# A blocked fast-multiplication kernel: five more operand pairs split a second time, A read in longer runs, and its first block weighed while it is staged

## The chip, the cores and the metric

The kernel runs on one core of a Trainium2 chip. The metric is device time in microseconds of one execution. Before the change it is 1574.9 us, the median of three runs (1574.21 to 1575.22). The profile shown below is of one further execution; its span is 1572.0 us.

The engines are named as in the profile: PE is TensorE (PEld its weight loads), DVE is VectorE, ACT is ScalarE, POOL is GpSimd, SP is SyncE.

## The reference

```python
def setup_inputs():
    m, k, n = 4096, 4096, 4096
    return {"a": np.random.randn(m, k).astype(np.float32),
            "b": np.random.randn(k, n).astype(np.float32)}

def reference(a, b):
    x = np.matmul(a, b)
    return 0.5 * x * (1 + np.tanh(np.sqrt(2 / np.pi) * (x + 0.044715 * x**3)))
```

A product of two 4096 x 4096 matrices, followed by the tanh form of GELU. Input and output are float32.

## The kernel before

A and B are cut in half both ways, into quadrants 11, 12, 21 and 22. Seven products of sums of quadrants (a Strassen scheme) give the four quadrants of the result, in place of eight. Everything is cast to float16 by the DMA that loads it; sums are accumulated in float32 in PSUM. The output is made in 16 groups: four blocks of rows of A (`mb`), each with four blocks of columns of B (`nb`). One group needs the seven products M1 to M7, each of 512 x 512 outputs over a depth of 2048. A product is done in four steps `q`, a step being 16 matmuls of 128 x 512:

```python
PRODUCTS = [   # name, chain of PSUM banks, operand of A, operand of B
    ("M3", "Y", "11", ("12", "22", 1)),
    ("M5", "X", ("11", "12", -1), "22"),
    ("M7", "X", ("12", "22", -1), ("21", "22", 1)),
    ("M1", "X", ("11", "22", -1), ("11", "22", -1)),
    ("M4", "X", "22", ("21", "11", 1)),
    ("M2", "Y", ("22", "21", -1), "11"),
    ("M6", "Y", ("21", "11", -1), ("11", "12", 1)),
]
```

In some groups a pair of products (M3 with M5, or M2 with M1) is split once more: the product's two operand blocks are cut in quarters, and seven products of quarter sums take the place of eight. One such small product is one step of 16 matmuls of 128 x 256 (with two of 128 x 512 in one of the seven). `FRESH` is the order of the seven products in groups where M2 and M1 are split. `SPLITS` says which groups split which pair:

```python
SPLIT = {"1": ("11", ("11", "22", -1), ("11", "22", -1)), "3": ("12", "11", ("12", "22", 1)), ...}
PAIR = [(s, p) for ps in ("213", "45", "76") for s in (0, 1) for p in ps]   # 14 steps, two chains in turn
SPLITS = {M3_M5: (11, 13, 14, 15), M2_M1: (13, 14)}

def multiply_split(gi, s, p):
    ...
    for r in range(RT // 2):
        ...
        for j in range(NJ):                                   # 2 x 8 matmuls
            wide = p == "2" and j == 0
            nc.tensor.matmul(
                banks[chain, i][:, :] if wide else out,
                sa[:, j // 2, r * P : (r + 1) * P, j % 2],
                sb[:, : NC] if wide else sb[:, j * NC // 2 : (j + 1) * NC // 2], ...)
    ...
    # joins of the small products: DVE additions and ACT copies of 128 x 256 float32
```

The split needs operands of its own. Of B, the quarter sums are made once for each column block in the group `maker[nb]`, written to DRAM (`k_split`) and fetched back by POOL's DMA in later groups (tile `bK`, 1 MB each). Of A, first the block's sum (`aD`, four DVE additions of 128 x 2048), then the quarters' sums from it (`aS`, one addition each). The instructions of each engine stand in the order in which this code records them; a `step` is the unit of this schedule, and lists such as `before[n]` and `tasks[n]` say what is recorded just before step `n`.

```python
def block_sum(gi, s, o, q):        # aD <- aT, aT
def operand_a(gi, s, q, tag):      # aS <- aD, aD  or  aS <- aT, aT
def make_split(gi, name, p):       # bS <- bK, bK, then keep_operand -> k_split in DRAM
    ...
            if block and q == PAIR[0][1]:                     # the four sums of a block, all in one step
                e = max(ready, last_a, *(e for _, e in places[s]))
                for qq in range(QPH):
                    task(e, block_sum, gi, s, oa, qq)
```

A is loaded into one of two buffers `stage`, in runs of 256 elements of a row, and turned by DVE's 32 x 32 transpose into `aT`. It is also weighed: the kernel takes the sums of squares of the rows of A (and of columns of B) to find out at the end whether float16 was safe; a general path stands behind it if not. ACT does this, one row of a tile at a time, with the squares written to a scrap tile. A block for later groups is staged by `stage_block` within the last group that uses the block before it (groups 3, 7 and 11). The first block is not weighed when it is loaded; it is read a second time for that, from group 9 on:

```python
a_v = a.rearrange("(x mm) (c g r) -> c g mm x r", mm=Q, g=4, r=RUN)      # RUN = 256

def load_a(mb, quad, c, h=None):
    s = pool.tile([P, NX, RUN], F16, name="stage", tag="stage", bufs=2)
    return [(s[g * Q : (g + 1) * Q, x : x + n, :], a_v[kh * CH + c, g, :, x0 : x0 + n, :]) for g in range(4)]

def weigh_rows(mb, quad, c, xs):
    for x in xs:
        nc.scalar.activation(weighed[mb, quad, c][:, :RUN], s[:, x, :], ACT.Square,
                             accum_out=weighed[mb, ih][:, k, x : x + 1])

def stage_block(mb, turns, turned=True):
    for (quad, c), n in zip(chunks, turns):
        do(max(n - LOAD_AHEAD, free_at.pop(0)), load, (load_a, (mb, quad, c)))   # LOAD_AHEAD = 6 steps
        do(n, turn_a, mb, quad, c)
        for x in range(3):
            do(n + 1 + x, weigh_rows, mb, quad, c, ...)
stage_block(0, [first_step[CHECK_GROUP] + 8 + 6 * x ...], turned=False)           # CHECK_GROUP = 9
```

At the start, group 0 runs on whatever has been loaded: 16 steps of plain products of quadrants (`plain`), then the second halves of M3, M5, M7 and so on. 46 matmuls on zeros (`warm`) come ahead of it. ACT copies finished sums out of PSUM in between: `keep("x1", ...)`, the tile `c21`, and `keep("m5", ...)`. The order of the loads and turns of the first block is a table:

```python
for n, whats in (
    (0, "A11_0 B12_0 T11_0 B11_0 A21_0 A12_0 B22_0 B21_0"),    # A, B: load; T: turn
    (4, "T21_0 A22_0"), (6, "T12_0"), (8, "A11_1+B12_1+B22_1"), (9, "T22_0 A12_1+B21_1a B21_1b"),
    (14, "T11_1 A22_1 B11_1"), (16, "T12_1 A21_1"), (18, "S2 S3 T22_1"), (23, "T21_1"),
):
```

Of the kernel before, what the change touches and what calls it, by code (L numbers as in the profile page):

```python
# [16 lines left out]
P = 128  # L17
# [45 lines left out]

MAKES = (("M3", (1, 0)), ("M5", (2, 1)), ("M1", (4, 0)), ("M2", (5, 3)))
M3_M5, M2_M1 = 0, 3
PLACE = {"M3": (M3_M5, 0), "M5": (M3_M5, 1), "M2": (M2_M1, 0), "M1": (M2_M1, 1)}
SPLIT_AHEAD = 6
FETCH_AHEAD = 12
SPLITS = {M3_M5: (11, 13, 14, 15), M2_M1: (13, 14)}
LOAD_AHEAD = 6  # L70
CHECK_GROUP = 9

TURNS = ((2, 2), (3, 3), (5, 2), (6, 2), (8, 0), (9, 0), (10, 2), (11, 2))
# [58 lines left out]
def half_path(  # L132
# [26 lines left out]
    checks = {which: iter(range(stats[which].shape[1] // NX)) for which in stats}  # L159

    a_v = a.rearrange("(x mm) (c g r) -> c g mm x r", mm=Q, g=4, r=RUN)
    b_v = b.rearrange("(c g jj q e) n -> c g e q jj n", g=4, q=Q, e=2, jj=NJ // 2)
# [6 lines left out]
    def load_a(mb, quad, c, h=None):  # L169

        ih, kh = int(quad[0]) - 1, int(quad[1]) - 1
        n = NX if h is None else NX // 2
        x = 0 if h is None else h * n
        x0 = (ih * MH + mb * TM) // Q + x
        if not h:
            s = pool.tile([P, NX, RUN], F16, name="stage", tag="stage", bufs=2)
            staged[mb, quad, c] = s
        s = staged[mb, quad, c]
        return [
            (s[g * Q : (g + 1) * Q, x : x + n, :], a_v[kh * CH + c, g, :, x0 : x0 + n, :])  # L180
            for g in range(4)
        ]

    def turn_a(mb, quad, c, h=None):
        if not h:
            t = pool.tile([P, NJ // 2, TM * 2], F16, name="aT", tag=f"aT{a_slot[quad]}{c}")
            a_tiles[mb, quad, c] = t
        s, t = staged[mb, quad, c], a_tiles[mb, quad, c]
        x = slice(0, NX) if h is None else slice(h * NX // 2, (h + 1) * NX // 2)
        src = s.bitcast(U32).rearrange("p mb (jj q) -> p jj mb q", q=Q)  # L190
        dst = t.bitcast(U32).rearrange("p jj (mb q) -> p jj mb q", q=Q)
        nc.vector.transpose(dst[:, :, x, :], src[:, :, x, :])  # L192
        if h != 0 and mb == 0:
            del staged[mb, quad, c]

    def load_b(nb, quad, c, h=None):
        kh, jh = int(quad[0]) - 1, int(quad[1]) - 1
        n0 = jh * NH + nb * NC
        if not h:
# [5 lines left out]
            (t[g * Q : (g + 1) * Q, e::2, :], b_v[kh * CH + c, g, e, :, :, n0 : n0 + NC])  # L205
# [23 lines left out]
    def weigh_rows(mb, quad, c, xs):  # L229

        ih, kh = int(quad[0]) - 1, int(quad[1]) - 1
        s = staged[mb, quad, c]
        if (mb, ih) not in weighed:
            weighed[mb, ih] = pool.tile([P, 2 * CH, NX], F32, name="rows", tag="rows")
        if xs[0] == 0:
            weighed[mb, quad, c] = pool.tile([P, RUN], BF16, name="scrap", tag="scrap")
        for x in xs:
            k = kh * CH + c
            nc.scalar.activation(  # L239
                weighed[mb, quad, c][:, :RUN], s[:, x, :], ACT.Square, accum_out=weighed[mb, ih][:, k, x : x + 1]  # L240
            )
        if xs[-1] == NX - 1:
            del weighed[mb, quad, c], staged[mb, quad, c]

    def weigh_half(mb, ih):
        k, t = next(checks["a"]), weighed.pop((mb, ih))
        nc.vector.tensor_reduce(
            out=stats["a"][:, k * NX : (k + 1) * NX],
            in_=t.rearrange("p k x -> p x k"), axis=AX.X, op=ALU.add,
        )  # L250

# [16 lines left out]
    def weigh():  # L268

        for half in sorted(energy):  # L270
            k, t = next(checks["b"]), energy[half]
# [27 lines left out]
    def verdict(row):  # L299

        t = pool.tile([P, RUN], BF16, name="verdict", tag="scrap").bitcast(F32)[0:1, :]
# [30 lines left out]
    def product(gi, s):  # L332
        if gi == len(groups) - 1:
            return LAST[s]
        return (FRESH if gi in SPLITS[M2_M1] else PRODUCTS)[s]
# [59 lines left out]

    N_RAW = NNB + 2
    last_raw = {nb: max(g for g in range(N_RAW) if groups[g][1] == nb) for nb in range(NNB)}
    maker = {nb: min(g for g in range(N_RAW, len(groups)) if groups[g][1] == nb) for nb in range(NNB)}
# [168 lines left out]
    def settle(gi, name, i):  # L567

        X, Y = banks.get(("X", i)), banks.get(("Y", i))
        end = gi == len(groups) - 1  # L570
# [86 lines left out]


    for n, whats in (
        (0, "A11_0 B12_0 T11_0 B11_0 A21_0 A12_0 B22_0 B21_0"),  # L660
        (4, "T21_0 A22_0"),
        (6, "T12_0"),
        (8, "A11_1+B12_1+B22_1"),
        (9, "T22_0 A12_1+B21_1a B21_1b"),
        (14, "T11_1 A22_1 B11_1"),
        (16, "T12_1 A21_1"),
        (18, "S2 S3 T22_1"),
        (23, "T21_1"),
    ):
        for what in whats.split():  # L670
            half = what[-1] == "0" and what != "A11_0" or what in ("A22_1", "T22_1")
            if what[0] == "S":
                before.setdefault(n, []).append((make_sums, (0, 2, int(what[1]), "bS")))
                continue
# [41 lines left out]
    chunks = [(quad, c) for quad in ("11", "12", "22", "21") for c in range(CH)]  # L716

    def stage_block(mb, turns, turned=True):
        def do(n, fn, *args):
            before.setdefault(n, []).append((fn, args))  # L720

        free_at = [0, 0]
        for (quad, c), n in zip(chunks, turns):
            do(max(n - LOAD_AHEAD, free_at.pop(0)), load, (load_a, (mb, quad, c)))
            free_at.append(n + 4)
            if turned:
                do(n, turn_a, mb, quad, c)
            for x in range(3):
                do(n + 1 + x, weigh_rows, mb, quad, c, list(range(NX))[x * 6 : (x + 1) * 6])
            if c == CH - 1 and quad in ("12", "21"):  # L730
                do(n + 4, weigh_half, mb, int(quad[0]) - 1)

    for gi in range(len(groups) - 1):
        if groups[gi + 1][0] != groups[gi][0]:
            stage_block(groups[gi + 1][0], [step_number(gi, s, q) for s, q in TURNS])
    stage_block(0, [first_step[CHECK_GROUP] + 8 + 6 * x for x in range(len(chunks))], turned=False)
# [113 lines left out]
    def open_block(gi, s, c, x):  # L850
        split_tiles["d", gi, s, c] = ring_tile(x, "aD")
# [38 lines left out]
    def make_split(gi, name, p):  # L890

        nb = groups[gi][1]
# [19 lines left out]

    def split_key(gi, s, p):
# [3 lines left out]
    def plan_fetch(units, key, n, ahead):  # L917
        if key not in units or owner[units[key]] != key:
            after = 0
            if key[2] == "split":  # L920
                after = 1 + max(made_at.get((nb, key[3], 2 * key[4] + x), -1) for x in range(2))
# [3 lines left out]

    for gi in range(N_RAW, len(groups)):
        nb = groups[gi][1]
        made = gi == maker[nb]
        mine = [n for n in range(first_step[gi], first_step.get(gi + 1, len(steps)))]
        ready = position[gi - 1, NP - 1, 2] if groups[gi][0] != groups[gi - 1][0] else 0  # L930
        units, places, users = {}, {}, {}

        makes = {}
        if made:
            for name, (s, q) in MAKES:
                s0, x = PLACE[name]
                for k, p in enumerate(p for p in SPLIT if not isinstance(SPLIT[p][2], str)):
                    n = step_number(gi, s, q) + k
                    makes.setdefault(n, []).append((name, p))
                    made_at[nb, s0, PAIR.index((x, p))] = n  # L940
        for n in mine:
            _, s, q = steps[n]
            name, _, oa, ob = product(gi, s)
            for made_name, p in makes.get(n, ()):
                for c in range(CH):
                    plan_fetch(units, (gi, nb, made_name, c), n, FETCH_AHEAD)
                task(n, make_split, gi, made_name, p)
# [4 lines left out]
            if block and q == PAIR[0][1]:  # L952
                places[s] = [ring_place(n, SPLIT_AHEAD, (gi, s, c)) for c in range(CH)]
                users[s] = []
                e = max(ready, last_a, *(e for _, e in places[s]))
                for c, (x, _) in enumerate(places[s]):
# [88 lines left out]
```

## Time and profile before

| | before |
|---|---|
| time, median of three | 1574.9 us |
| span of the profile | 1572.0 us |
| PE busy | 1553.1 us (99%), 7822 records |
| PE weight loads busy | 766.1 us (49%) |
| DVE busy | 1112.0 us (71%) |
| ACT busy | 670.1 us (43%) |
| POOL busy | 391.2 us (25%) |
| DMA | 418.88 MB in 219780 packets, mean 266 GB/s |
| granted PE clock | 0.998 |

The page gives each engine's busy time and share of the span first. Matmuls overlap each other in the records (one is recorded with about 380 ns), so the pace of the PE is read from the distance between the starts of rows in the timeline, and its stops from the waits. A timeline row is: start, duration, engine, line, operation, output and inputs, count, and in brackets the idle time before it with what ended it.

### The profile page before, as it was taken

Reading aid. Unit: us, or ns where it says so; the run is one execution under the profiler, and the core shown is the slowest. Engines: PE = TensorE matmul, PEld = TensorE weight load, DVE = VectorE, ACT = ScalarE, POOL = GpSimd, SP = SyncE. Lnnn points to the kernel's source line nnn. Section 1 sums busy time; section 2 is a strip of 40 time slices with the busy share of each in tenths; the row PEclk is TensorE's granted clock in tenths of the full one; section 3 lists DMA queues with packets and bytes.
Section 4 is the critical chain, followed back from the end, with each engine's and each line's share of the span. In section 5 each row is a group of like instructions: output and inputs, shape, how many; then the busy total and the mean of one; then the engine's idle time right before and its main releaser. Section 6 shows DMA issues by size and latency. Waiting matters only on the chain. (4 is left out here: it accounts for less than half of the span.)

```text
span 1572.0 us, 21821 instructions
## 1 busy us (share of the span) xinstructions
PE 1553.1 (99%) x7822; PEld 766.1 (49%) x7822; DVE 1112.0 (71%) x1281; ACT 670.1 (43%) x1670; POOL 391.2 (25%) x682
## 2 busy tenths in 40 slices
PE   9999999999999999999999999999899999999998
PEld 4444444444444444444444444444644457677653
DVE  1697988969888886776755557577654668688853
ACT  1036444338874641212566345563356733232211
POOL 7763433331124300011222112121222111212100
PEclk9999999999999999999999999999999999999999
DMA  9999999994799986799999789998999856978852
GB/s 175 197 217 296 265 318 268 287 201 79 202 228 294 296 321 243 306 324 315 330 339 302 229 277 332 354 353 270 365 279 291 229 173 239 322 257 296 297 211 82
DMA packets 219780, 418.88 MB, mean 266 GB/s; under 512 B 18192, under 2 KB 141072, under 8 KB 200464
## 3 DMA queue, kind: packets, MB, share of 16 engines
q0 software_dynamic: 157024, 249.60, 66.5%
q1 hardware_dynamic: 62640, 167.81, 28.5%
q8 instruction: 63, 1.03, 0.3%
q14 instruction: 53, 0.43, 0.1%
HBM read 333.45 MB, written 167.78 MB: 319 GB/s over the span
## 5 line engine op out<-in xcount | busy, mean ns | idle before, releaser
L418 PEld LDWEIGHTS <-aS 128*128 128x128 f16 x4448 | 435.5, 98 | 533.8 <-issue 7.1
L418 PE MATMUL accX<-bK,aS 128*128 128x512 f16 x1664 | 362.9, 380 | 4.0 <-ACT x L529 4.0
L418 PEld LDWEIGHTS <-aT 128*128 128x128 f16 x1728 | 169.1, 98 | 205.1 <-issue 1.8
L832 DVE TENSOR_TENSOR aS<-aT 128x2048 f16<-128x2048 f16 x188 | 223.2, 1217 | 58.2 <-PE accX L418 47.1
L239 ACT ACTIVATE scrap<-stage 128x256 bf16<-128x256 f16 x512 | 212.8, 416 | 50.1 <-DMA stage<-in_a_dram 35.6
L556 ACT ACTIVATE y<-y 128x512 f32<-128x512 f32 x192 | 119.0, 630 | 270.0 <-DVE y L565 269.9
L217 POOL DMA_DIRECT2D bR<-in_b_dram x320 | 173.2, 543 | 208.5 <-DMA bR<-in_b_dram 117.7
L418 PE MATMUL accY<-bK,aS 128*128 128x512 f16 x1024 | 222.3, 379 | 0.0
L818 POOL DMA_DIRECT2D bK<-k_M x116 | 62.5, 541 | 449.3 <-PE accX L418 121.8
L217 POOL DMA_DIRECT2D stage<-in_a_dram x176 | 111.6, 640 | 240.2 <-ACT scrap L239 188.7
L378 DVE TENSOR_TENSOR aS<-aT 128x2048 f16<-128x2048 f16 (+1 forms) x112 | 133.8, 1199 | 32.3 <-PE accX L418 23.4
L418 PE MATMUL accX<-bS,aS 128*128 128x512 f16 x704 | 153.4, 379 | 1.9 <-DVE bS L378 1.2
L378 DVE TENSOR_TENSOR bS<-bR 128x2048 f16<-128x2048 f16 x110 | 133.6, 1217 | 18.0 <-PE accX L418 9.6
L261 ACT ACTIVATE square<-bR 128x1024 bf16<-128x1024 f16 x120 | 123.0, 1049 | 50.5 <-DVE energy L565 50.3
L529 ACT COPY x<-accX 128x512 f32<-128x512 f32 x120 | 69.5, 586 | 153.4 <-PE accX L418 147.3
L529 ACT COPY m<-accX 128x512 f32<-128x512 f32 x68 | 39.2, 582 | 187.1 <-PE accX L418 175.3
L192 DVE STREAM_TRANSPOSE aT<-stage 128x2048 uint32<-128x2048 uint32 (+1 forms) x37 | 74.5, 2017 | 62.6 <-DMA stage<-in_a_dram 56.5
L832 DVE TENSOR_TENSOR bS<-bK 128x2048 f16<-128x2048 f16 x80 | 96.9, 1216 | 28.6 <-DMA k_split<-bS 28.6
L418 PE MATMUL accY<-bK,aT 128*128 128x512 f16 x512 | 111.8, 379 | 0.0
L418 PE MATMUL accX<-bK,aT 128*128 128x512 f16 x512 | 111.8, 379 | 0.0
L500 PEld LDWEIGHTS <-aS 128*128 128x128 f16 x960 | 93.9, 98 | 17.2 <-issue 2.5
L239 ACT ACTIVATION_READ_ACCUMULATOR scrap<-stage 128x1 f32 x512 | 95.6, 187 | 0.0
(70 smaller groups left out, 1302.9 us busy)
## 6 DMA issues: line engine op xcount, KB each, us to landing
bK<-k_M POOLq DMA_DIRECT2D x116, 1024.0 KB, 11.5
out_dram<-y SPq DMA_DIRECT2D x256, 256.0 KB, 6.6
bR<-in_b_dram POOLq DMA_DIRECT2D x320, 128.0 KB, 7.7
k_M<-bS SPq DMA_DIRECT2D x80, 512.0 KB, 6.7
k_split<-bS SPq DMA_DIRECT2D x80, 512.0 KB, 7.7
stage<-in_a_dram POOLq DMA_DIRECT2D x144, 256.0 KB, 12.3
bK<-k_split POOLq DMA_DIRECT2D x18, 1024.0 KB, 6.6
k_M<-bR SPq DMA_DIRECT2D x16, 1024.0 KB, 12.2
```

Source lines behind the costliest of these rows:

```text
L192: nc.vector.transpose(dst[:, :, x, :], src[:, :, x, :])
L217: nc.gpsimd.dma_start(out=dst, in_=src)
L239: nc.scalar.activation(weighed[mb, quad, c][:, :RUN], s[:, x, :], ACT.Square, accum_out=weighed[mb, ih][:, k, x : x + 1])
L261: nc.scalar.activation(t[:, :], src, ACT.Square)
L378: nc.vector.tensor_tensor(out=x, in0=y, in1=z, op=ALU.add if o[2] > 0 else ALU.subtract)
L418: nc.tensor.matmul(acc[:, :], sa[:, j // 2, i * P : (i + 1) * P, j % 2], sb[:, j, :], start=start and j == 0, stop=stop and j == 3, skip_g ...
L500: nc.tensor.matmul(banks[chain, i][:, :] if wide else out, sa[:, j // 2, r * P : (r + 1) * P, j % 2], sb[:, : NC] if wide else sb[:, j * N ...
L529: nc.scalar.copy(out=t[:, :], in_=src[:, :])
L556: nc.scalar.activation(y[:, :], src[:, :], ACT.Gelu_apprx_tanh)
L818: nc.gpsimd.dma_start(out=t, in_=kept_unit(*key[1:])[:, :])
L832: nc.vector.tensor_tensor(out=t, in0=y, in1=z, op=ALU.add if op > 0 else ALU.subtract)
```

## The change

It has four parts.

1. **Splits.** M3 with M5 is split in groups 9 and 10 as well, and M2 with M1 in 9, 10 and 15, so that groups 9, 10, 13, 14 and 15 have all four chains of both pairs split, and 11 has one pair. The quarter sums of B are made at places named one by one (`MAKES`), in groups 6, 7, 8 and 12 that split nothing, in place of each column block's first later group.
2. **A's sums.** A split block's sum for M2 and M1 (`STAY`) is made once for a block of rows and kept for the following groups that split the same product; that of M2 lies in the two `stage` buffers. The DVE additions are spread over steps with little other DVE work (`sum_step`), not all recorded in one.
3. **A in runs of 512.** The contraction index is mapped so that both chunks of a quadrant lie next to each other in a row of A; for the blocks after the first one, one load takes 512 elements of a row for half of the rows.
4. **Weighing.** ACT's squares are written over the staged tile itself, so the scrap tile goes, but the buffer `stage` is free only when the weighing is done. The first block is weighed when it is loaded (entries `W` in the table), so that its second reading goes. The rows of the other blocks are weighed 512 elements at a time.

```diff
-MAKES = (("M3", (1, 0)), ("M5", (2, 1)), ("M1", (4, 0)), ("M2", (5, 3)))
+MAKES = (
+    (6, 0, 3, 1, "M3"), (6, 2, 0, 1, "M5"), (6, 3, 1, 3, "M3"), (6, 4, 2, 3, "M5"), (6, 5, 3, 3, "M1"),
+    (7, 0, 3, 3, "M2"), (7, 2, 3, 0, "M3"), (7, 4, 0, 0, "M5"), (7, 5, 3, 0, "M1"),
+    (8, 1, 2, 2, "M3"), (8, 2, 3, 2, "M5"), (8, 5, 0, 0, "M2"), (12, 2, 0, 2, "M1"), (12, 4, 0, 2, "M2"),
+)
+STAY = ("M2", "M1")
+STAY_AHEAD = 20
+BLOCK_AHEAD = 12
-SPLITS = {M3_M5: (11, 13, 14, 15), M2_M1: (13, 14)}
+SPLITS = {M3_M5: (9,10,11,13,14,15), M2_M1: (9,10,13,14,15)}
-CHECK_GROUP = 9
-TURNS = ((2, 2), (3, 3), (5, 2), (6, 2), (8, 0), (9, 0), (10, 2), (11, 2))
+TURNS = ((2, 2), (3, 3), (5, 2), (6, 2), (7, 2), (8, 1), (10, 1), (11, 1))
 ... cut ...
-    a_v = a.rearrange("(x mm) (c g r) -> c g mm x r", mm=Q, g=4, r=RUN)
+    a_v = a.rearrange("(x mm) (h g s) -> h g mm x s", mm=Q, g=4, s=CH * RUN)
 ... cut: B's index is mapped the same way ...
+    def load_half(mb, quad, h):
+        s = pool.tile([P, NX, RUN], F16, name="stage", tag="stage", bufs=2)
+        s = staged[mb, quad, h] = s.rearrange("p (x c) r -> p x (c r)", c=CH)
+        return [(s[g * Q : (g + 1) * Q, :, :], a_v[kh, g, :, x0 : x0 + n, :]) for g in range(4)]
+    def turn_half(mb, quad, h):
+        for c in range(CH):
+            turn_a(mb, quad, c, h)
+    def weigh_row(dst, src):
+        nc.scalar.activation(src, src, ACT.Square, accum_out=dst)
 ... cut ...
     def product(gi, s):
-        if gi == len(groups) - 1:
-            return LAST[s]
-        return (FRESH if gi in SPLITS[M2_M1] else PRODUCTS)[s]
+        if gi in SPLITS[M2_M1]:
+            return FRESH[s]
+        return (LAST if gi == len(groups) - 1 else PRODUCTS)[s]
 ... cut ...
-        (0, "A11_0 B12_0 T11_0 B11_0 A21_0 A12_0 B22_0 B21_0"),
-        (4, "T21_0 A22_0"),
-        (6, "T12_0"),
+        (0, "A11_0 B12_0 T11_0 W11_0 B11_0 A21_0 A12_0 B22_0 B21_0"),
+        (4, "T21_0 W21_0 A22_0"),
+        (6, "T12_0 W12_0"),
         (8, "A11_1+B12_1+B22_1"),
-        (9, "T22_0 A12_1+B21_1a B21_1b"),
-        (14, "T11_1 A22_1 B11_1"),
-        (16, "T12_1 A21_1"),
+        (9, "T22_0 W22_0 A12_1+B21_1a B21_1b"),
+        (14, "T11_1 W11_1 A22_1 B11_1"),
+        (16, "T12_1 W12_1:0-4"),
+        (17, "W12_1:4-16 A21_1"),
+        (34, "W22_1:0-1"), ... one row a step to (65, "W21_1:15-16"),
 ... cut ...
-    stage_block(0, [first_step[CHECK_GROUP] + 8 + 6 * x for x in range(len(chunks))], turned=False)
+            at_step(max(n - LOAD_AHEAD, free_at.pop(0)), load, (load_half, (mb, quad, h)))
+            at_step(n, turn_half, mb, quad, h)
+            for x in range(2):
+                at_step(n + 1 + x, weigh_rows, mb, quad, h, list(range(NX // 2))[x * 4 : (x + 1) * 4])
 ... cut ...
+    def sum_step(need, first):
+        fit = {n: (work.get(n, 0) + 1) / (1.5 if steps[n][2] in SPLIT else 3) for n in range(first, need)}
+        e = next((n for n in fit if fit[n] <= 1), min(fit, key=fit.get) if fit else need)
+        add_work(e, 1)
+        return e
 ... cut ...
+    def plan_block(gi, s, n):
+        twins = [g for g in SPLITS[PLACE[name][0]] if groups[g][0] == mb and g >= gi]
+        first = max(n - (STAY_AHEAD if name in STAY else BLOCK_AHEAD), ready(mb, oa))
+        ...
+        for q in range(QPH):
+            e = sum_step(n, e)
+            task(e, block_sum, gi, s, oa, q)
```

## The prediction

> **What bounds the kernel now.** I read the busy shares first, then the PE's timeline for its pace, then the PE's waits, and last the other engines' timelines around the two places where the PE stood still longest.
>
> ```profile
> PE 1553.1 (99%) x7822; PEld 766.1 (49%) x7822; DVE 1112.0 (71%) x1281; ACT 670.1 (43%) x1670; POOL 391.2 (25%) x682
> ...
> PE accX L418 <- ACT x L529: 4.7, 2, 4.0
> PE accX L500 <- DVE y L565: 2.4, 1, 2.4
> PE accY L418 <- DVE y L565: 1.8, 2, 1.4
> PE accY L418 <- DVE bS L378: 1.5, 1, 1.5
> ```
>
> The first line says that only fewer or faster matmuls can move this kernel far. The others (waits of the PE: total us, times, longest) are nearly all of its idle time; with the small rows that I leave out it is 13.6 us, of which 1.4 us lie ahead of the first matmul. So 12.2 us is all that a better schedule could return, and the number of matmuls is the rest.
>
> The pace comes from the starts of neighbouring timeline rows:
>
> ```profile
> 13.93 7.07 PE L449 MATMUL accY<-bR,aT 128*128 128x512 f16 x32
> 20.84 7.07 PE L449 MATMUL accX<-bR,aT 128*128 128x512 f16 x32
> ...
> 1111.82 3.66 PE L500 MATMUL accY<-bK,aS 128*128 128x256 f16 x32
> 1115.32 3.66 PE L500 MATMUL accX<-bK,aS 128*128 128x256 f16 x32
> 1118.81 13.98 PE L418 MATMUL accX<-bK,aS 128*128 128x512 f16 x64
> 1136.79 5.56 PE L418 MATMUL accX<-bK,aS 128*128 128x512 f16 x18 [4.01 <-ACT x L529]
> ```
>
> (20.84 - 13.93)/32 = 0.216 us for a matmul of 512 columns, (1118.81 - 1111.82)/64 = 0.1092 us for one of 256. The narrow ones cost 1.2% over half, and are not held up by their weight loads. A sum checks this. The code has 480 matmuls in group 0 and 448 in each other group; six split pairs replace 6 x 128 wide ones by 6 x (4 wide + 220 narrow). That is 6456 x 0.216 + 1320 x 0.1092 = 1538.6 us, plus 13.9 us before the first real one, 12.2 us of stops, some 1.7 us of lowered clock (the granted clock is 0.83 in the 10 us from 1135, after the long stop) and 5.2 us from the last matmul to the end: 1571.6, against a span of 1572.0. Nothing is hidden elsewhere.
>
> The last row is the longest stop, 4.0 us, in group 11. ACT shows why:
>
> ```profile
> 1120.46 1.23 ACT L556 ACTIVATE y<-y 128x512 f32<-128x512 f32 x2 [0.27 <-DVE y L565]
> 1133.06 0.42 ACT L239 ACTIVATE scrap<-stage 128x256 bf16<-128x256 f16 x1 [11.37 <-DMA stage<-in_a_dram]
> ...
> 1136.18 2.02 ACT L529 COPY x<-accX 128x512 f32<-128x512 f32 x4
> ```
>
> ACT stood 11.4 us at the weighing of a tile of A that had not landed; six rows (3.1 us) went ahead of the copy that the PE needed. The tile's load was sent at 1111.4 and the loads around it took 14.5 to 19.4 us to land, because fetches of B's operands filled the queue; group 11 is the only one that both splits and stages, and a split step lasts half as long, so six steps ahead are less time.
>
> **What the Trainium skill says.** "TensorE: Matmul & The Clock Gate", Back-to-back issue gap: N/2.4 + 2.5 ns when warm, which is 215.8 and 109.2 ns; the trace has 216 and 109.2. The same page, Part 1, says an idle window of some 3.4 us halves the clock; the trace agrees with its 0.83 after 4.0 us. "Perfetto Trace Analysis", Per-instruction lifecycle, calls ACT and DVE strict FIFO; the 11.4 us above are this. "DMA: Bandwidth & Descriptors", Why small descriptors are slow, names a fixed overhead for each packet; the windows fit it: from 10 to 20 us, with A and B cast in short runs, the DMA engines are 1.24 busy at 201 GB/s, from 1110 to 1115, with fetches of B's operands, 1.03 at 424 GB/s.
>
> **The change part by part.**
>
> *Matmuls.* Five more pairs (groups 9 and 10 both, 15 one). Each removes 124 x 0.216 = 26.78 us and adds 220 x 0.1092 = 24.02 us, so it saves 2.76 us; five save **13.8 us**, all on the path.
>
> *DVE.* Counting instructions in both programs: `aS` from `aD` 40 to 80, `aD` 32 to 40, `aS` from `aT` 296 to 274, `bS` from `bK` 80 to 70, together 16 more of 1.217 us = 19.5 us. Joins 96 to 176 of 0.42 us = 33.6 us. Turns: 24 of 2.304 us become 48 of 1.240 us, 4.2 us. In all +57 us: DVE goes to about 1165 us, 75%. By group, adding the rows' durations, group 9 has most of the new work, 80 us of DVE in 91 us of matmuls; groups 13 and 14 had 77 and 79 before and did not stop the PE. Beside other work: 0 on the path, with 1.5 us for small stops in the new split groups (the one of 2.4 us in the waits is such a stop, at the start of group 11).
>
> *ACT.* 512 weighings of 416 + 187 ns become 128 of these and 192 of twice the width. Between 416 ns for 256 and 1049 ns for 1024 elements, 512 comes to 627 ns, with the 187 to 0.81 us: 309 to 233 us. Against that, 40 more small copies (0.375 us) and 28 more large ones (0.585 us) add 31 us. ACT falls by some 44 us. Off the path.
>
> *DMA.* `bK` grows from 158 to 193 MB, because products made in another block's group fetch their sources separately. The second reading of the first block goes (8.4 MB as float16), 5 MB less are written to `k_split`: about 20 MB more on 419. Off the path unless a fetch is late.
>
> *Staging in group 11.* The same bytes in half as many packets. If the load lands 3 us earlier, near 1130, the four rows of 0.81 us end at 1133.3, and the PE, which needs the copy at 1132.4, waits some 1.5 us, too short for the clock to fall. Of 4.0 + 1.7 us I count **4.2 us** back. The spread sums should also take the stop of 2.4 us at that group's start: 1.5 us back.
>
> *The start.* Here the change adds to a crowded stage.
>
> ```profile
> 29.67 0.58 ACT L465 COPY c<-accY 128x512 f32<-128x512 f32 x1 [8.05 <-PE accY L449]
> ...
> 81.37 0.58 ACT L529 COPY m<-accX 128x512 f32<-128x512 f32 x1 [45.94 <-PE accX L418]
> ...
> 70.15 1.15 POOL L217 DMA_DIRECT2D stage<-in_a_dram  x2 [1.05 <-DMA stage<-in_a_dram]
> ...
> 78.67 1.23 DVE L192 STREAM_TRANSPOSE aT<-stage 128x1024 uint32<-128x1024 uint32 x1
> ```
>
> ACT is idle for 45.9 us, and the new weighings fit in, 16 rows = 9.65 us a chunk. But they stand ahead of copies in ACT's order, and they hold the buffer. Chunk 21 is turned at 24.7 and 27.4 us, so its weighing ends near 35.7 and the four `c` copies, done one by one from 29.67 until now, follow it; the PE wants the first bank back at 35.4 and gets it near 36.3: 0.9 us. Chunks 12 and 22 then run to 57.5. Chunk 11_1 is turned by 65.5 and weighed until 75.15, and only then is the buffer free for 22_1, whose load is sent at 70.15 today. Sent at 75.2 it lands near 80 and 82.6 where the turns stand at 78.67 and 81.27: DVE loses about 1.5 us. Chunk 12_1 is weighed until 84.8, ahead of the `m` copies of 81.37, and M7 waits for these at 83.8 + 0.9: another 0.7 us. DVE is busy nearly without a break from 72 to 119 us, so a loss there comes through to the PE, but it is the same 1.6 us, not another. With 1 us for ACT's rows between the squares of group 1: **2.6 us lost**.
>
> *The end.* The last group takes the `FRESH` order and ends with M6, whose sum needs a DVE addition (0.68 us) between matmul and GELU; M7 needed none. **0.7 us lost.**
>
> Sum: -13.8 - 4.2 - 1.5 + 1.5 + 2.6 + 0.7 = -14.7 us, so 1574.9 becomes 1560.2. I take 1560.5.
>
> **The rivals.**
>
> 1. *The buffer becomes the bound at the start.* For it: POOL sends in order, so a load that waits for ACT holds B's loads behind it, and the DMA engines run dry for 2 us or more. Against it: most loads land 5 us after they are sent, a cushion. It would lose 5 to 8 us in place of 2.6: 1563 to 1566.
> 2. *DVE takes over in the split groups.* For it: 80 of 91 us in order, and each new split start can cost 2.4 us. Against it: groups 13 and 14 at the same load, and the change spreads the sums. Five such stops and a few smaller ones, 12 us, would leave 1571.
> 3. *Fetches of B come late.* For it: 424 GB/s in the split stage of group 11, and 35 MB more. Against it: no PE wait on `bK` in the whole trace, and groups 13 and 14 fetch 20 MB each at a mean below 280 GB/s. It would add a few us in groups 6, 7 and 10 (18, 20 and 22 MB).
> 4. *Staging was worth more.* If the stops of group 11 and of groups 0 to 4 all go, 1553.
>
> **Range and chances.** The matmul term is sure to half a us. The uncertain terms are the start (0 to 8 us), group 11 (0 to 5.7 us back) and new stops (0 to 8 us); together 1554 to 1568. A gain of 2% needs 31.5 us, more than the 13.8 and all 12.2 us of stops together; a loss of 2% needs stops of 45 us.
>
> **What would show it.** Narrow matmuls 1320 to 2420 and wide ones down by 620; starts still 0.216 and 0.1092 us apart; PE busy near 1540. ACT's waits for `stage` in group 11 shorter than 11.4 us and the clock there at 1.00. In the first 90 us a PE wait on an ACT copy of about 1 us, and the load of chunk 22_1 released by ACT near 75 us. DVE near 75%. I am wrong if split groups show repeated PE waits on DVE or on `bK`, or if the wait on ACT at the start is many us.

## The result and the profile after

The changed kernel takes **1595.2 us** (median of four runs, 1590.8 to 1600.2), against 1574.6 us for the kernel before beside it: a ratio of 1.0133, with a 95% interval of 1.0101 to 1.0166. It is slower by about 21 us. The prediction was 1560.5 us with a range to 1568, so it lies far outside the range, in the wrong direction. The span of the profiled execution is 1589.3 us.

First the page of the changed kernel: the busy shares, three rows of the 40 slices (39.7 us each), and the DMA total.

```profile
PE 1546.0 (97%) x8302; PEld 813.4 (51%) x8302; DVE 1162.5 (73%) x1401; ACT 616.7 (39%) x1354; POOL 401.5 (25%) x705
...
PE   9999999999999999979978999999999999999998
...
PEclk9999999999999999999989999999999999999999
DMA  9999999994899986999999998597999988778693
...
DMA packets 184792, 442.00 MB, mean 278 GB/s; under 512 B 18401, under 2 KB 100321, under 8 KB 163553
```

The share of the PE fell from 99% to 97%, and apart from the last slice the three under 9 are the 18th, 21st and 22nd: 675 to 715 us and 795 to 874 us. They lie at the ends of groups 6 and 7 and in group 8 (by the count of matmuls, the three groups run from 611 to 936 us). None of these groups splits anything: they stage A or make quarter sums of B. Every other part of the kernel runs close to full.

The PE's waits (total us, times, longest us):

```profile
PE accY L448 <- DVE y L595: 12.2, 3, 8.3
PE accY L448 <- DMA bK<-k_M: 9.5, 2, 6.6
PE accX L448 <- DVE aS L897: 7.8, 2, 5.5
PE accX L448 <- DVE bS L410: 4.4, 3, 2.1
```

The second row is a wait that the kernel before doesn't have at all: the PE waits for a fetch of B's operands. The first and third name DVE. Of the first row, 8.3 us are the longest stop of all, in group 6; what DVE waited for there is in the timeline, first DVE and then the PE. (A row: start, duration, engine, line, operation, output and inputs, count, and in brackets the idle time before with what ended it.)

```profile
699.23 1.22 DVE L897 TENSOR_TENSOR bS<-bK 128x2048 f16<-128x2048 f16 x1 [8.97 <-DMA k_split<-bS]
700.37 1.22 DVE L897 TENSOR_TENSOR aS<-aT 128x2048 f16<-128x2048 f16 x1
701.50 2.48 DVE L595 TENSOR_TENSOR y<-x,accY 128x512 f32<-128x512 f32 x4
...
702.24 15.91 PE L448 MATMUL accY<-bK,aS 128*128 128x512 f16 x64 [8.29 <-DVE y L595]
```

DVE's next quarter sum of B needs a buffer `bS`, and this is free only when the write of an earlier quarter sum to DRAM (`k_split`) has landed. DVE waited 9.0 us for it. DVE keeps its order, so the operand of A and the four additions that empty the bank `accY` stood behind it, and the PE stood still for 8.3 us. In the 22 us from 680 to 702 such a write of 512 KB took 16.9 us from issue to landing (median of four); the fastest of the eleven between 660 and 712 us took 3.2 us.

The third row is two stops of group 8, and has another origin: DVE stood for 9.4 and 9.1 us at transposes of A whose load had not landed, and the operand `aS` stood behind them. The later one, DVE and then the PE:

```profile
855.25 2.37 DVE L203 STREAM_TRANSPOSE aT<-stage 128x1024 uint32<-128x1024 uint32 x2 [9.11 <-DMA stage<-in_a_dram]
...
859.92 6.31 PE L448 MATMUL accX<-bK,aS 128*128 128x512 f16 x21 [5.46 <-DVE aS L897]
```

So the PE stopped in three ways, behind a late write, a late fetch of B's operands and a late load of A, and each is a transfer.

Why were they late? The windows of group 6 (busy times of PE, PEld, DVE, ACT and POOL, then the granted clock of the PE, the DMA share and GB/s):

```profile
604.00:614.00 10.00, 10.00 (x48) 4.58 (x47) 9.37 (x15) 2.52 (x4) 1.06 (x2) 1.00 1.02 394
614.00:624.00 10.00, 10.00 (x48) 4.51 (x47) 4.67 (x5) 0.00 (x0) 0.00 (x0) 1.00 0.81 325
624.00:634.00 10.00, 10.00 (x48) 4.49 (x46) 4.53 (x4) 0.00 (x0) 0.00 (x0) 1.00 0.14 54
...
664.00:674.00 10.00, 10.00 (x48) 4.58 (x47) 8.44 (x11) 2.12 (x4) 1.53 (x3) 1.00 1.02 427
674.00:684.00 10.00, 10.00 (x48) 4.50 (x47) 7.42 (x9) 2.39 (x4) 1.11 (x3) 1.00 1.01 408
684.00:694.00 10.00, 9.95 (x47) 4.41 (x45) 5.86 (x5) 0.00 (x0) 1.58 (x3) 1.00 1.03 379
694.00:704.00 10.00, 1.76 (x5) 0.65 (x5) 4.77 (x7) 1.73 (x3) 0.53 (x1) 0.77 1.01 424
```

and the kernel before in the same stretch, where it too makes quarter sums in group 6:

```profile
664.00:674.00 10.00, 10.00 (x49) 4.52 (x47) 8.42 (x10) 0.00 (x0) 0.53 (x1) 1.00 0.64 212
674.00:684.00 10.00, 10.00 (x48) 4.58 (x47) 6.17 (x7) 2.39 (x4) 1.58 (x3) 1.00 0.91 324
684.00:694.00 10.00, 10.00 (x48) 4.49 (x47) 8.45 (x10) 2.49 (x4) 0.00 (x0) 1.00 0.99 404
694.00:704.00 10.00, 10.00 (x49) 4.51 (x47) 5.90 (x6) 0.74 (x2) 0.53 (x1) 1.00 0.86 296
```

In the changed kernel the DMA engines have almost nothing to do from 624 to 634 us, and from 644 to 704 us they have no free moment: the last four rows have a share of 1.0 at 379 to 427 GB/s. The mean from 604 to 711 us, 351 GB/s, hides both. "DMA: Bandwidth & Descriptors", Specifications, in the Trainium skill gives 435 GB/s as the ceiling of the fabric; 427 is the most that the windows quoted here show. The kernel before has a share of 0.64 to 0.99 at that point, and its PE does not stop.

The pause at 624 us has its reason in POOL:

```profile
604.63 1.10 POOL L883 DMA_DIRECT2D bK<-k_M  x2 [7.03 <-DVE bS L410]
634.71 1.05 POOL L883 DMA_DIRECT2D bK<-k_M  x2 [28.97 <-DVE bS L897]
```

The tiles `bK` form a ring of eight places, and POOL could not send the next fetch for 29 us because no place was free. The kernel before has a pause of 36 us there without a stop, so the pause alone does no harm; it has less to move afterwards.

Adding up what the starts of neighbouring matmuls exceed the nominal 0.216 and 0.1092 us (lowered clock included), the PE loses 45.7 us in the changed kernel against 15.2 before, and 35.3 of the 45.7 are in groups 6 to 8 (10.4, 12.9 and 12.0), where the kernel before loses nothing. Counted from the two programs, the fetches of `bK` and the writes of quarter sums in these three groups are 30.5, 30 and 24.5 MB (of 2^20 bytes) after, 85 in all, and 21, 23 and 17 before, 61 in all (one or two fetches at the border of two groups may be counted to either).

### The profile page after: what moved, and what is told of

Read it like the earlier page. It is cut to its first block, busy times and chain, and to the rows that moved or that the text cites. A ratio compares the mean times of both kernels' runs of the same rounds, so it can differ in the third digit from the quotient of the medians.

```text
span 1589.3 us, 22718 instructions
## 1 busy us (share of the span) xinstructions
PE 1546.0 (97%) x8302; PEld 813.4 (51%) x8302; DVE 1162.5 (73%) x1401; ACT 616.7 (39%) x1354; POOL 401.5 (25%) x705
## 5 line engine op out<-in xcount | busy, mean ns | idle before, releaser
L448 PEld LDWEIGHTS <-aS 128*128 128x128 f16 x3936 | 386.1, 98 | 504.5 <-issue 34.0
L448 PE MATMUL accX<-bK,aS 128*128 128x512 f16 x1536 | 335.8, 380 | 7.8 <-DVE aS L897 7.8
L253 ACT ACTIVATE stage<-stage 128x512 f16<-128x512 f16 (+1 forms) x320 | 169.4, 531 | 148.8 <-DVE aT L203 133.2
L897 DVE TENSOR_TENSOR aS<-aT 128x2048 f16<-128x2048 f16 x166 | 197.6, 1218 | 40.0 <-PE accX L448 35.6
L530 PEld LDWEIGHTS <-aS 128*128 128x128 f16 x1760 | 172.1, 98 | 27.5 <-DVE aS L897 0.5
L448 PE MATMUL accY<-bK,aS 128*128 128x512 f16 x640 | 144.7, 388 | 19.9 <-DVE y L595 10.4
L410 DVE TENSOR_TENSOR bS<-bR 128x2048 f16<-128x2048 f16 x110 | 133.7, 1218 | 18.7 <-PE accX L448 10.3
L203 DVE STREAM_TRANSPOSE aT<-stage 128x1024 uint32<-128x1024 uint32 (+1 forms) x61 | 76.0, 1278 | 86.0 <-DMA stage<-in_a_dram 77.9
L239 POOL DMA_DIRECT2D stage<-in_a_dram x144 | 84.6, 593 | 149.6 <-ACT stage L253 114.4
L530 PE MATMUL accX<-bK,aS 128*128 128x256 f16 (+1 forms) x880 | 104.0, 275 | 0.2 <-DVE aS L897 0.2
L530 PE MATMUL accY<-bK,aS 128*128 128x256 f16 (+1 forms) x880 | 103.8, 275 | 0.0
L897 DVE TENSOR_TENSOR aS<-aD 128x2048 f16<-128x2048 f16 x80 | 95.3, 1218 | 1.7 <-PE accX L448 0.8
```

The source lines that it names most:

```text
L203: nc.vector.transpose(dst[:, :, x, :], src)
L239: nc.gpsimd.dma_start(out=dst, in_=src)
L253: nc.scalar.activation(src, src, ACT.Square, accum_out=dst)
L410: nc.vector.tensor_tensor(out=x, in0=y, in1=z, op=ALU.add if o[2] > 0 else ALU.subtract)
L448: nc.tensor.matmul(acc[:, :], sa[:, j // 2, i * P : (i + 1) * P, j % 2], sb[:, j, :], start=start and j == 0, stop=stop and j == 3, skip_g ...
L530: nc.tensor.matmul(banks[chain, i][:, :] if wide else out, sa[:, j // 2, r * P : (r + 1) * P, j % 2], sb[:, : NC] if wide else sb[:, j * N ...
```

## The experiments

Each ratio is against the kernel before, run on the same chip, with its 95% interval. The theory: **traffic in groups 6 to 8**, that is, fetches and writes for the quarter sums, saturates the DMA engines, writes land late, and DVE and the PE wait. Of the 14 makes, 10 are of another column block than the group's own. Such a make has to fetch its two sources only for itself (20 MB in all, 16 of them in groups 6 to 8), where a make of the group's own block takes tiles that the product needs anyhow. Rivals: the places of the ring (what is fetched holds a place, whatever its size); weighing of the first block; squares written over the staged tile, which hold `stage` longer; too short a lead of the loads.

### The source fetches alone, the writes alone

`no_source_fetch` leaves out the fetches for makes of another block. The sums are made of tiles of A that lie in SBUF, so the values are other ones, and the time is that of the same instructions:

```diff
-                for c in range(CH):
+                for c in range(CH) if make[0] == nb else ():      # plan_fetch of a make's sources
-        blocks = [split_tiles[gi, nb, name, c] for c in range(CH)]
+        blocks = ... if nb == own else [a_tiles[mb, quad, c] for c in range(CH)]
```

> The changed kernel, but where quarter sums are made in a group of another column block, they are made from tiles of A that lie in SBUF, in place of fetched tiles of B: the result of the split groups is another one, every DVE addition and every write to DRAM stays, 20 MiB of fetches go. Groups 6, 7, 8 then move 25.5, 22 and 21.5 MiB in place of 30.5, 30 and 24.5. Theory 1: stops in groups 6 to 8 fall from 37 to under 10 us, time 1556 to 1568. Theory 2 (writes and buffers alone): 25 us or more of the stops stay, 1580 or more. Theory 3: groups 7 and 8 keep most of theirs, 1578 or more.

Measured: **1558.4 us**, ratio 0.9907 (0.9887 to 0.9926). The PE's losses fall from 45.7 to 12.2 us, with none in groups 6 to 8. Its windows of these groups (each begins some 8 us ahead of its group):

```profile
604.00:701.00 97.00, 97.00 (x451) 43.93 (x449) 71.94 (x77) 16.43 (x28) 7.40 (x14) 1.00 0.87 332
701.00:799.00 98.00, 98.00 (x455) 44.41 (x454) 70.09 (x72) 31.29 (x76) 19.32 (x34) 1.00 1.06 346
799.00:896.00 97.00, 97.00 (x451) 44.01 (x450) 72.36 (x76) 41.33 (x108) 16.10 (x27) 1.00 0.99 315
```

From the first matmul of one group to that of the next, the three groups take 96.7 us each, in place of 107.1, 109.6 and 108.8, with all the instructions of DVE and ACT, all the writes and all the splits. POOL's pause of 29 us, up to 636.5 us, is there too and does no harm. So 37 us of the result come with these fetches; without them the time is 2 us from the prediction.

`short_writes` keeps the fetches and writes only an eighth of each quarter sum; the later fetches take other data of the same size:

```diff
-        keep_operand((nb, "split", s0, k // 2), k % 2, t[:, :])
+        nc.sync.dma_start(out=dst, in_=t[:, : NC // 2])            # an eighth of the columns
```

> The changed kernel, but only an eighth of each quarter sum is written to DRAM, and the split groups fetch a product's operand of the same size in its place: the result of the split groups is another one, all fetches and DVE additions stay, 31 MiB of writes go; groups 6, 7, 8 move 19.6, 21.2 and 17.9 MiB. Theory 1: stops in groups 6 to 8 fall to under 8 us, 1555 to 1566. Theory 2 says the same here, as the buffers come free early. Theory 3: groups 7 and 8 keep over 15 us of stops.

Measured: 1561.3 us, ratio 0.9930 (0.9908 to 0.9952), and no loss in groups 6 and 7; 5.8 us stay in group 8. So cutting 26 of the 30 MB of writes in groups 6 to 8 does nearly what cutting 16 MB of fetches does: neither is too much by itself, their sum is. Shorter writes also free the buffers `bS` sooner, so this run alone doesn't part the bytes from the wait for a buffer; `no_source_fetch`, with every write and the same buffers, does.

### Makes in the block's own group

`own_makes` keeps the parts of the change that have to do with A, and puts every make into a group that has that column block (6: two, 7, 9 and 10: four each), which allows seven split pairs:

```diff
-    (6, 0, 3, 1, "M3"), (6, 2, 0, 1, "M5"), (6, 3, 1, 3, "M3"), ...
+    (6, 1, 0, 1, "M3"), (6, 2, 1, 1, "M5"), (7, 1, 0, 2, "M3"), (7, 2, 1, 2, "M5"), ...
-SPLITS = {M3_M5: (9,10,11,13,14,15), M2_M1: (9,10,13,14,15)}
+SPLITS = {M3_M5: (11, 13, 14, 15), M2_M1: (13, 14, 15)}
```

> The changed kernel, but groups 9 and 10 split nothing, and each column block's quarter sums are made in a group of that block (6, 7, 9, 10), so that one fetch of a product's operand serves the product and the making of its quarter sums. Fetches fall from 193 to 161 MiB, and in groups 6, 7 and 8 fetches and writes of quarter sums together from 30.5, 30 and 24.5 to 18, 21 and 17 MiB. Theory 1 (added fetches saturate the DMA engines in groups 6 to 8, writes of quarter sums land late, DVE and then the PE wait): the stops of groups 6 to 8 (some 37 us with the lowered clock) go nearly all, four split pairs fewer give back 11 us: 1562 to 1570. Theory 2 (too many quarter sums for three buffers, whatever the traffic): group 7 still makes four products and keeps about 8 us of stops: 1570 to 1576. Theory 3 (A in halves, with the buffer held by the weighing, starves groups 7 and 8): their stops of some 27 us stay: 1590.

Measured: 1577.3 us, ratio 1.0027 (1.0014 to 1.0040). The long stops of groups 6 and 7 are gone, as the theory says, but the time is outside every range that was expected, 7 us above the theory's. In the traced execution, at 1582.5 us the slowest of the eight, the losses are in groups 4, 8, 11 and 12 (6.1, 5.1, 4.3 and 2.7 us), all next to staging of A, and one stop of group 11 that the prediction called cured is back in part (the third row):

```profile
PE accX L459 <- DVE aS L908: 4.6, 2, 3.3
PE accX L459 <- DVE bS L421: 4.3, 3, 2.1
PE accX L459 <- ACT x L570: 2.5, 1, 2.5
```

So the parts that have to do with A don't pay what I had counted. `own_makes_no_weigh` takes the weighing of the first block out of it (the sums of squares are set to a constant):

```diff
-        for x in xs:
-            weigh_row(stats["a"][:, k : k + 1], staged[0, quad, c][:, x, :])
+        return
```

> As own_makes, but the first block of A is not weighed at all (its statistics are set to a constant): it leaves out 128 rows of ACT work in groups 0 and 1 and frees the staging buffers at the transpose. If the weighing costs what was forecast, the start is 2.6 us shorter than with it: the time is 2 to 3 us under own_makes. If it is hidden, as the stops of the first 160 us suggest (4.8 us before, 6.0 us after), 0.5 to 1.5 us under it.

Measured: 1578.9 us, ratio 1.0030 (1.0016 to 1.0044), no gain over the kernel with the weighing. The two intervals together leave room for a gain of some 2.5 us, so a cost of the size forecast is unlikely, but not excluded.

### The change with another order of blocks

If the makes' own groups are good places, and late groups are wanted for splits, the order of the column blocks can be changed: `reordered` takes the blocks 3, 1, 2, 0 with the third block of rows and 0, 1, 2, 3 with the fourth, makes blocks 1, 2 and 3 in their own groups 6, 7 and 8, and splits both pairs in 9, 10, 13, 14 and 15: ten pairs, against eleven in the change and six before. Nothing of the computation is left out.

```diff
+        order = {2: [3, 1, 2, 0], 3: [0, 1, 2, 3]}.get(mb, order)
-    (6, 0, 3, 1, "M3"), (6, 2, 0, 1, "M5"), ...
+    (6, 1, 0, 1, "M3"), (6, 2, 1, 1, "M5"), (6, 4, 0, 1, "M1"), (6, 5, 3, 1, "M2"), (7, 1, 0, 2, "M3"), ...
-SPLITS = {M3_M5: (9,10,11,13,14,15), M2_M1: (9,10,13,14,15)}
+SPLITS = {M3_M5: (9,10,13,14,15), M2_M1: (9,10,13,14,15)}
```

> The changed kernel with the column blocks of the last two blocks of rows in another order (3, 1, 2, 0 and 0, 1, 2, 3), so that groups 9, 10, 13, 14 and 15 still split all four chains, and every quarter sum is made in a group of its own column block, from the fetch that the product needs anyway (groups 6, 7 and 8, four products each); group 11 splits nothing. Ten pairs are split in place of eleven. Fetches and writes of quarter sums in groups 6, 7, 8: 21, 23 and 24 MiB in place of 30.5, 30 and 24.5; three buffers, DVE additions and the staging of A as in the changed kernel. Theory 1: no long stop in groups 6 and 7, a few us in 8: 1558 to 1566. If three buffers or A in halves were the cause, 1575 or more.

Measured: **1567.8 us** (1565.3 to 1570.0), ratio 0.9965 (0.9953 to 0.9978), 2 us above the range expected. It beats both kernels, by 0.35% and 1.7%. Fetches and writes are 21, 23 and 24 MB in groups 6 to 8, and the windows show groups 6 and 7 without a stop, and one left in 8:

```profile
604.00:701.00 97.00, 97.00 (x452) 43.86 (x450) 65.85 (x71) 16.42 (x28) 6.68 (x13) 1.00 0.78 296
701.00:799.00 98.00, 98.00 (x456) 44.35 (x455) 69.94 (x71) 32.84 (x81) 19.16 (x34) 1.00 1.04 334
799.00:912.00 113.00, 107.08 (x498) 49.01 (x497) 83.61 (x87) 42.44 (x110) 18.10 (x30) 0.97 0.95 309
```

Group 8 has four makes and stages A's next tiles. What is left there comes from A, as its DVE row shows: the transposes waited 8.8 us for their load, and the operand `aS` behind them was late.

```profile
827.27 2.37 DVE L212 STREAM_TRANSPOSE aT<-stage 128x1024 uint32<-128x1024 uint32 x2 [8.79 <-DMA stage<-in_a_dram]
```

### Putting the suspected cost back

`reordered_extra` adds fetches that nobody reads, two of 1 MB for each of the eight makes of groups 6 and 7 (16 MB; some 7 MB are sent within each of the two groups, the rest ahead of them); all else is `reordered`:

```diff
                     plan_fetch(units, (gi, *make[:2], c), n, FETCH_AHEAD)
+                    if gi in (6, 7):
+                        plan_fetch(units, (gi, (nb + 2) % NNB, make[1], c), n, FETCH_AHEAD)
```

> As reordered, but in groups 6 and 7 each made product's operand of a second column block is fetched too, and not used: 7 MiB more in each of the two groups (28 and 30 MiB), no other instruction is added. Theory 1: the stops of groups 6 to 8 come back, 10 us in group 6 and 10 to 20 us in 7 and 8: 1578 to 1595. If traffic is not the cause: as reordered.

Measured: **1606.3 us**, ratio 1.0207 (1.0187 to 1.0228): 38.5 us more than `reordered`, for 16 MB, and more than the 1578 to 1595 expected. The losses are 9.5, 25.2 and 10.8 us in groups 6 to 8, against 0, 0 and 8.6. The PE's waits and the windows:

```profile
PE accX L458 <- DMA bK<-k_M: 21.7, 2, 14.3
PE accX L458 <- DVE aS L907: 8.5, 2, 7.5
PE accY L458 <- DMA bK<-k_M: 6.3, 1, 6.3
```

```profile
630.00:640.00 10.00, 10.00 (x48) 4.51 (x46) 6.89 (x7) 1.46 (x3) 0.00 (x0) 1.00 0.27 107
640.00:650.00 10.00, 7.72 (x36) 3.43 (x35) 9.37 (x10) 2.89 (x6) 2.62 (x5) 1.00 0.78 256
650.00:660.00 10.00, 4.91 (x14) 1.82 (x14) 0.40 (x1) 0.00 (x0) 0.00 (x0) 0.66 1.01 418
```

In the first of these windows the DMA engines are three quarters idle: POOL sends nothing from 608 to 644 us, as the places of the ring are taken. Then four fetches go out together and a fifth 4 us later, and the PE stands. `reordered` has the same pause of 36 us, sends two fetches after it and one more 4 us later, and doesn't stop. What follows the pause can hurt by its bytes or by the places that it takes, and the next two runs part the two.

### Bytes or places of the ring

Both keep the fetches that are in dispute, at the same points of the program and in the same places, and let each carry an eighth of its bytes. `slots_kept` does so with the change's own source fetches (sums made from A, as in `no_source_fetch`), `reordered_slots` with the unused fetches of `reordered_extra`.

```diff
+    def fetch_part(key, x):
+        t = split_tiles[key] = ring_tile(x, "bK")
+        nc.gpsimd.dma_start(out=t[:, :NC], in_=kept_unit(*key[1:])[:, :NC])
-            task(e, fetch, key, units[key])
+            task(e, fetch if key[2] == "split" or key[1] == groups[key[0]][1] else fetch_part, key, units[key])
```

> The changed kernel with every fetch at its place in the ring of eight tiles and the ring's order unchanged, but where a product's operand is fetched only to make quarter sums of another column block, an eighth of it is fetched, and the quarter sums are made from tiles of A in SBUF (the split groups' result is another one). Bytes of no_source_fetch within 2 MiB, ring of the changed kernel. Theory 1 (bytes: the DMA engines are saturated): as no_source_fetch, 1556 to 1564, no long stop in groups 6 and 7. Theory 1b (slots: the extra fetches hold places of the ring, so that other fetches are sent late and all at once): stops of 15 us or more stay, 1575 to 1595.

Measured: 1571.7 us, ratio 0.9986 (0.9977 to 0.9995). It stands between: of the 36.8 us from 1595.2 to 1558.4, 23.5 go with the bytes and 13.3 stay with the places. Groups 6 and 7 have no stop any more; what stays in the trace is in group 8, 10.3 us, where a load of A goes out at 817.4 us that `no_source_fetch` sends at 809.6. Neither theory's range holds the result.

> As reordered_extra, with an eighth of each unused fetch: the ring's places are taken as there, 12 MiB of the 14 MiB of added bytes are not moved. reordered_extra left the DMA engines at 0.28 from 620 to 640 us and sent five fetches at once at 644. Theory 1 (bytes): within 4 us of reordered, 1566 to 1572. Theory 1b (slots): 20 us or more above reordered, 1588 to 1606.

Measured: 1584.8 us, ratio 1.0071 (1.0048 to 1.0094). It too lies between the two ranges. Of the 38.5 us that the unused fetches cost, 17.0 stay with the places and 21.5 go with the bytes. The two pairs agree that both count: somewhat over half goes with the bytes; the rest stays with the places, most likely because a place taken by one fetch delays the sending of others. No run frees the places and keeps the bytes, so these parts hold for this order of taking away. The share of the places is a lower bound in the first pair, since no sum reads these tiles, and a place may come free sooner than in the change.

### Rivals on the side of A

`reordered_scrap` and `own_makes_scrap` write the squares of the third and fourth blocks of rows to a scrap tile, as the kernel before does, in place of over `stage`:

```diff
+                nc.scalar.activation(z[:, : CH * RUN], staged[mb, quad, h][:, x, :], ACT.Square, accum_out=...)
```

> As reordered, but for the third and fourth blocks of A the squares of the weighing go to a scrap tile, as in the kernel before, and not over the staged tile, so that ACT need not wait for DVE's transposes. If writing in place is what costs in groups 7, 8, 11 and 12, stops there shrink by 3 to 8 us and the time is 3 to 8 us lower than reordered; if it is the arrival of A or DVE's order, within 2 us of it.

Measured: 1570.6 us, ratio 0.9975 (0.9964 to 0.9985), no gain over `reordered`, and 8.8 us lost in group 8 as against 8.6.

> As own_makes, with the same scrap tile for the third and fourth blocks of A. own_makes has 3.8, 2.8 and 2.7 us of stops in groups 8, 11 and 12 where the kernel before has 0, 6.9 and 0. If writing in place causes them: groups 8 and 12 fall under 1 us, time 1571 to 1574; if not, 1575 to 1579 as own_makes.

Measured: 1576.6 us, ratio 1.0013 (1.0003 to 1.0024). Its median lies within the spread of `own_makes` (1574.8 to 1582.5). In the one trace of each, group 8 loses 1.1 us in place of 5.1, but group 12 loses 7.2 in place of 2.7. Writing in place costs nothing in the time that these runs can show.

`reordered_ahead8` and `own_makes_ahead8` send the loads of A eight steps ahead instead of six:

```diff
-LOAD_AHEAD = 6
+LOAD_AHEAD = 8
```

> As reordered, with A's loads sent up to 8 steps ahead of their turn in place of 6, where the buffer is free. reordered has 6.5 us of stops in group 8, where DVE stands 10.8 us at a transpose whose tile has not landed, and 4.5 us in group 4. If the lead is what lacks, these fall under 5 us together and the time is 4 to 7 us below reordered, 1561 to 1564; if the buffers, free only after the weighing, set the time of the loads, within 2 us of reordered.

Measured: 1573.0 us, ratio 0.9995 (0.9986 to 1.0004): some 5 us slower than `reordered`.

> As own_makes, with A's loads up to 8 steps ahead. own_makes has stops in groups 8, 11 and 12 (9.3 us) and 4 (4.6 us). If the lead of A's loads is what lacks, 1566 to 1571; if not, 1575 to 1579. In group 11 the first load should then land before ACT's copy needs its place in the order.

Measured: 1581.4 us, ratio 1.0047 (1.0031 to 1.0063), not faster than `own_makes`, whose interval (1.0014 to 1.0040) overlaps. In its trace the stops of groups 11 and 12 (7.0 us in `own_makes`) are gone, so in those two groups the lead did lack. The gain doesn't show in the time: groups 0 and 1, where the two programs are the same, happen to lose 11.7 us in this trace, as against 6.6. So a longer lead makes `reordered` worse and `own_makes` no better, and as the general cause of the losses it falls.

**What stays open:** why `own_makes` loses 2.7 to 6.1 us in each of groups 4, 8, 11 and 12. Neither the weighing of the first block, nor squares in place, nor the lead explains it as a whole. Group 4 loses 4.0 to 6.1 us in every one of the thirteen traces of kernels that stage A as the change does, against 2.2 in groups 3 and 4 together before; the prediction has no term for it. The new table of turns and the loads in halves were not parted. More `bS` buffers, the direct remedy for DVE's wait on a write, were not tried.

## Why the prediction was wrong

- **Matmuls: right.** Wide ones fell by 620 and narrow ones rose by 1100, the starts are still 0.216 and 0.109 us apart. 13.8 us are saved, and in `no_source_fetch`, with the same matmuls, they come through to the time.
- **DVE in the split groups (+1.5): right in kind.** Groups 9, 10 and 13 to 15 lose 0.4 us together; DVE is at 1162.5 us (1165 predicted). Rival 2 didn't come.
- **ACT (-44 us): right in kind.** It fell by 53; a weighing of 512 elements takes 617 ns (627 estimated).
- **The start (2.6 lost): not settled.** The load of chunk 22_1 waits for ACT and goes out at 72.6 us, in place of 70.15, for the reason given (near 75 was predicted). In its trace the PE loses 1.2 us more than before in groups 0 and 1, of which 0.4 us is a wait for a copy `m`. But the twelve traces with this same start lose from 4.5 to 11.7 us there, against 4.8 in the one of the kernel before, so one trace doesn't tell 1.2 from 2.6. `own_makes_no_weigh` shows no gain from taking the weighing away.
- **Group 11 (4.2 + 1.5 back): it came, and more; the reason given is not shown.** Its stops went, 8.2 us in all with the lowered clock, and the loads of A in groups 11 and 12 did land earlier, in 9.6 us (median) as against 11.9 before. But `own_makes`, with the same runs of 512, has a stop of 2.5 us at ACT there, and its loads take 17.4 us. So the longer runs do not by themselves land earlier.
- **The end (0.7 lost): right.** 6.1 us from the last matmul's start to the end of the span, against 5.6.
- **Packets: read too strongly.** The 201 GB/s at the start, as against 424 in group 11, were read as the cost of short packets. The windows count a cast load by the float16 that arrives: the page of the kernel before has 333.45 MB read from HBM and 249.60 MB on the queue of the loads, and the difference, 83.85 MB, is the half that the cast drops from the loads of A and B. Counted as read, the start moves about twice the 201 GB/s, so most of the difference is the cast. No run parts what is left.
- **DMA ("about 20 MB more on 419. Off the path unless a fetch is late"): this step failed.** The total was right, 442 MB against 439. The line counts bytes over the whole kernel, and rival 3 counts only fetched ones over whole groups ("18, 20 and 22 MB"), finds the mean of groups 13 and 14 below 280 GB/s, and gives the risk a few us. Three things were left out. The makes' *writes* fall into the same groups (12.5, 10 and 7.5 MB in groups 6, 7 and 8), so the sum is 30.5, 30 and 24.5 MB. A mean over a group hides that the ring holds fetches back and then lets them go at once; at 420 GB/s for tens of us there is nothing in reserve. And the trace before already had the first half of the link from a late write to the PE: DVE's `bS` waits ten times for the write of an earlier one, 28.6 us in all, and the bank's additions stand behind it. I had read only the PE's own waits on `bK`. Groups 6 to 8 cost 35.3 us where the sum had 0, and without the fetches made only for other blocks nothing is lost there.

With what the trace shows in place of each term, the sum of the spans closes: 1572.0 - 13.8 (matmuls) + 1.2 (start) - 8.2 (group 11) + 0.5 (end) + 1.8 (group 4) + 0.4 (group 9) + 35.3 (groups 6 to 8) = 1589.2, against a span of 1589.3. That `no_source_fetch` comes within 2 us of the prediction is partly luck: in its trace the stops of group 11 give back 2.5 us more than was counted, and group 4, which was not counted, takes 2.1.

Rival 3 was the right mechanism, in the right place for groups 6 and 7, with a size many times too small; for group 10, which only fetches, it was wrong. The longest single stop doesn't even go back to a fetch but to a write.

## What to carry to other kernels

When a change moves transfers, count reads and writes together for each stage, set the sum against the best rate that the trace shows (here about 420 GB/s) and not against its mean, and look for pauses in the sending: after a pause the same bytes have less time. In these runs a ring's place had a cost of its own beside the bytes (13 of 37 us and 17 of 38.5); a fetch that serves one helper only takes both. Follow each engine's queue one step back: a DVE that waits for a *write* to land is how DMA traffic reaches the PE without any wait on a fetch being in the list.

## What the hardware showed that I had not expected

- How a stop becomes more than its length: after the stop of 8.3 us the next ten matmuls start 0.427 us apart in place of 0.216, after which the pace is back; after 5.5 and 6.6 us the next eight do. After one of 2.9 us (803.88) seven start at full pace and the next eight 0.427 us apart, and after one of 2.3 us (843.92) none do. That is 1.5 to 1.9 us more for each of the four. "TensorE: Matmul & The Clock Gate", Part 1, in the Trainium skill names an idle window of about 3.4 us for this, which runs freely and doesn't start with the kernel. The three long stops agree with it, and a slowdown that begins 1.3 us after a stop agrees with a window whose place is not tied to the stop. The stop of 2.9 us is shorter than the window and still brought the slow pace, so in this trace the window was not idle throughout.
- The landing time of a transfer under load: by the fit in "DMA: Bandwidth & Descriptors", Anatomy of one DMA, in the Trainium skill, a fetch of 1 MB is estimated at 2.0 + 2.4 = 4.4 us; the median of the 116 such fetches of `bK` from `k_M` is 9.7 us in the changed kernel, and 8.2 in `reordered`:

```profile
bK<-k_M POOLq DMA_DIRECT2D x116, 1024.0 KB, 9.7
```
